# Hymba layer on one core: sums of weight blocks by adding DMAs instead of GpSimd operations, and roots by one GpSimd power

## Chip, cores and metric

The kernel runs on one core of a Trainium2 chip. The metric is the device time of one execution, in microseconds (us). The profile names the engines PE (TensorE; PEld is its weight loading), DVE (VectorE), ACT (ScalarE), POOL (GpSimd) and SP (SyncE, which here only issues DMAs).

## The reference, cut to what matters

One decoder layer for 1024 tokens of width 1024, in fp32: half a SwiGLU feed-forward network (FFN1), a mixer of a gated convolution and a diagonal state-space model (SSM), half a second FFN, each behind an RMSNorm with a shift, a scale and a gate from a condition vector.

```
x <- x + 1/2 * g1 * SwiGLU_1( adaLN_1(RMSNorm(x)) )          # d_ff = 2816
h  = adaLN_2(RMSNorm(x));  [b, c, v, u] = split(h @ W_in)
yA = b * conv3_causal(c * v)
yB = GLU( Re(C . state) + D*u ),  state_t = Abar state_{t-1} + Bbar u_t
x <- x + g2 * ( [RMSNorm(yA) | RMSNorm(yB)] @ W_out )
x <- x + 1/2 * g3 * SwiGLU_2( adaLN_3(RMSNorm(x)) )
y  = RMSNorm_final(x)

swiglu(h) = (silu(h @ w_gate) * (h @ w_up)) @ w_down
rms_norm(x) = x * rsqrt(mean(x * x) + 1e-6) * gain
```

## The kernel before

**Products.** Features lie on the 128 partitions, tokens on the columns in two halves of 512. Each fp32 operand is split into a high and a low part, and a product is three matmuls: high by high, high by low, low by high (`mm3`, 3 matmuls of 512 columns). A weight block of 128 x 1024 (512 KB, here called a granule) is split by ACT, which copies the high part, and DVE, which subtracts it (`w<-raw` in the profile). A granule feeds 24 matmuls in the FFNs.

**Seven instead of eight.** The FFN works in 11 groups of 256 hidden features. Most groups, and most of the down projection, are done as products of 2 x 2 blocks with seven block products instead of eight (`seven` for gate and up, `down7` for down). That is so for 9 groups of FFN1, 10 of FFN2, and 2 x 2 parts of the down projection in each FFN: 27 sets of seven. With left blocks A11, A12, A22 and sums of left blocks S1 to S4, the right operands are, of the four weight blocks of a set:

```
0: b11    1: b12 - b11    2: b22 - b12 + b11    3: b21
4: b22 - b12    5: b22    6: b21 - (b22 - b12 + b11)
```

Four of the seven are sums, and each takes one POOL operation over 128 x 1024 (lines 170, 171, 172 and 191). The first three are issued together, at the second granule of a set, from two raw tiles that hold two blocks each, partly in place; the fourth behind the split of the fifth granule. The tuple `SEVEN` gives the order of the products; banks B, C and A in PSUM collect them, and `copied`, `add`, `out` and `update` take them out by ACT and DVE.

**The weight stream.** `Weights` hands the granules out in a fixed list. SP loads raw tiles of 1 MB (two granules) into 2 buffers (`rawp`); split tiles go into a ring of 3 (`ringp`), with a fourth (`ring1`) at the head and in the mixer, where no `sums` tile is open. `pump` splits the next granule as soon as a tile of the ring is given back by `free`, and `ahead` loads the next raw tile when one is used up.

**The order.** All engines work off their instructions in order. The text of the kernel sets that order together with a scheduler that sorts by priority; `InOrder` (whose `call` is the line 112 of most instructions of PE, ACT, DVE and SP in the profile) ties each engine's instructions to the order in which they are written. `Clock` counts the `mm3` and lets side work in between them: in FFN1 the preparation of the SSM (`ssm_base`, `ssm_batch`: tables, and the kernels `kc` with the diagonal `dg` added, in 8 batches of 4 groups of channels), the modulation vectors (`wm`), and norms. `fa5gB` is bank B of gate in group 5 of FFN1, `fb0d` the down projection of group 0 of FFN2, `n_0` and `n_256` the halves of the last part of the final norm.

In the mixer a batch of the SSM goes through DVE (`X`, `sz`, `si`, `co`); `swx` and `swz` are pairs of small DMAs by SP that move states across partitions, and `yy` is the output on PE, which needs `co` after `swz` has landed.

**Roots.** `roots` makes 1/sqrt from sums of squares in a few columns per 128 tokens: a first guess from the bits (`ni`) and refinement, ten small DVE operations with the mean; `wide` spreads it over 128 columns times 0.375 (`rb`), and PE turns that into rows (`bc`). The squares themselves are added up by POOL in 8 pieces per norm (line 347).

Of the kernel before, what the change touches and what calls it, by code (L numbers as in the profile page):

```python
# [21 lines left out]
P = 128  # L22
# [22 lines left out]
PAD = 96, 100  # L45
# [10 lines left out]
ROOT_BITS, ROOT_A, ROOT_B = 1595932665.0, 0.703952253, 2.38924456  # L56
# [64 lines left out]
class Weights:  # L121
# [5 lines left out]
    def __init__(self, engines, srcs, granules, raw_bufs):  # L127
        self.V, self.A, self.SP, self.G = engines
        self.srcs, self.granules, self.raw_bufs = srcs, granules, raw_bufs
        self.left = [0] * len(srcs)  # L130
        for j, c, _ in granules:
            self.left[j] += c != "t4"
        self.raws, self.tiles, self.sums, self.kinds = [], [], {}, []
        self.given = self.freed = 0
        self.sums_pool = None
        self.slots = deque()

    @staticmethod
# [8 lines left out]
    def retire(self, pool):  # L147

        self.slots = deque(p for p in self.slots if p is not pool)
        self.kinds = [None if p is pool else p for p in self.kinds]  # L150
# [13 lines left out]
    def chunk(self, j, c, k):  # L164
        if isinstance(c, int):
            return self.raws[j][:, c, :]
        if c == "t1":
            f = self.sums[j] = self.sums_pool.tile([P, 1024], F32, tag="sums", name=f"sums{j}")
            b11, b12, b22 = self.raws[j][:, 0, :], self.raws[j][:, 1, :], self.raws[k][:, 0, :]
            self.G.tensor_tensor(out=f[:], in0=b22, in1=b12, op=ALU.subtract)  # L170
            self.G.tensor_tensor(out=b12, in0=b12, in1=b11, op=ALU.subtract)  # L171
            self.G.tensor_tensor(out=b11, in0=f[:], in1=b11, op=ALU.add)  # L172
        return {"t1": self.raws[j][:, 1, :], "t2": self.raws[j][:, 0, :]}.get(c, self.sums[j][:])

    def pump(self):
        while self.slots and len(self.tiles) < len(self.granules):
            i = len(self.tiles)
            j, c, k = self.granules[i]
            if self.sums_pool is None and c == "t1":
                return  # L180
            self.load((k if c == "t1" else j) + 1)
            src = self.chunk(j, c, k)
# [10 lines left out]
            self.left[j] -= c != "t4"  # L193
            self.ahead()

    def take(self, n=1):
        self.pump()
        got = self.tiles[self.given : self.given + n]
        assert len(got) == n
        self.given += n  # L200
        return got

    def free(self, n=1):
        for pool in self.kinds[self.freed : self.freed + n]:
            if pool is not None:
                self.slots.append(pool)
        self.freed += n
        self.pump()
# [9 lines left out]
def hymba_layer(ctx: ExitStack, tc, x_d, xt_d, wm1_d, wmod_d, gu1_d, gs1_d, ds1_d, wl1_d, win_d, wout_d, glu_d, gu2_d, gs2_d, wd2_d, ds2_d, wl2_d, cols_d, cond_d, lam_d, bc_d, out_d):  # L218
# [13 lines left out]
    ringp = pool("ringp", bufs=3, side="right")  # L232
    rawp = pool("rawp", bufs=2, side="right")
# [27 lines left out]
    V.memset(one[:], 1.0)  # L261
    mods = const.tile([P, 3, KT], F32, name="mods")
    scl = const.tile([P, 3, KT], F32, name="scl")
    gate = const.tile([P, 3, KT], F32, name="gate")

    srcs, granules = [], []

    def plain(arrays):
        for a in arrays:
            granules.extend((len(srcs), q, None) for q in range(2))  # L270
            srcs.append(a)

    def stream(gu, gs, wd, ds, wl, m):
# [4 lines left out]
        for g in range(m, NGRP):  # L278
            j = len(srcs)
            inner = g == 1  # L280
            srcs.extend([gs[g - m, 0], wd, gs[g - m, 1]] if inner else [gs[g - m, 0], gs[g - m, 1]])
            first, *rest = Weights.seven(j, j + 1 + inner)
            granules.extend([first, *([(j + 1, q, None) for q in range(2)] if inner else []), *rest])
        for c in range(CHUNKS):
            for p in range(2):
                granules.extend(Weights.seven(len(srcs), len(srcs) + 1))
                srcs.extend([ds[c, p, 0], ds[c, p, 1]])
# [5 lines left out]
    ws = Weights((V, A, SP, nc.gpsimd), srcs, granules, 2)  # L293
    ws.raw_pool = lambda i: rawp
# [79 lines left out]
    def roots(st, q, width, nm):  # L374

        v, y, a = (const.tile([P, 8], F32, tag=f"n{i}", name=f"{nm}n{i}", bufs=1)[:, :q] for i in "vya")
        yi = const.tile([P, 8], I32, tag="ni", name=nm + "ni", bufs=1)[:, :q]
        V.tensor_scalar(out=v, in0=st[:, :q], scalar1=1.0 / width, scalar2=EPS, op0=ALU.mult, op1=ALU.add)
        V.tensor_scalar(out=yi, in0=v.bitcast(I32), scalar1=-0.5, scalar2=ROOT_BITS, op0=ALU.mult, op1=ALU.add)
        src = yi.bitcast(F32)  # L380
        V.scalar_tensor_tensor(out=a, in0=src, scalar=-ROOT_A, in1=src, op0=ALU.mult, op1=ALU.mult)
        V.tensor_tensor(out=a, in0=a, in1=v, op=ALU.mult)
# [1482 lines left out]
```

## Time and profile before

| | |
|---|---|
| median of 3 runs | 1706.53 us (1703.99 to 1710.12) |
| profiled execution | 1708.08 us |
| its span in the trace | 1706.2 us, granted clock 0.991 |
| PE busy | 1668.5 us, 98% |
| DVE, ACT, POOL busy | 70%, 39%, 20% |
| the four sums on POOL, 27 times each | 70.0 + 73.7 + 71.9 + 66.6 us |
| DMA | 281.45 MB, 46% of the queues' time |

How to read the rows: in a row of the timeline the first number is the start in us after the span's start, the second the length (of a run of like instructions, with its count behind x), then the engine, the line, the operation, and out<-in with shapes. A bracket gives the idle time of the engine just ahead of it and what ended that. In rows of a window stand its bounds and length, busy time and count of PE, PEld, DVE, ACT and POOL, then PEclk, the clock that PE was granted (1.00 is full), then the DMA share and GB/s. Rows of grouped instructions end with busy us, mean ns of one, and the idle time before them.

### The profile page before, as it was taken

Reading aid. Unit: us, or ns where it says so; the run is one execution under the profiler, and the core shown is the slowest. Engines: PE = TensorE matmul, PEld = TensorE weight load, DVE = VectorE, ACT = ScalarE, POOL = GpSimd, SP = SyncE. Lnnn points to the kernel's source line nnn. Section 1 sums busy time; section 2 is a strip of 40 time slices with the busy share of each in tenths; the row PEclk is TensorE's granted clock in tenths of the full one; section 3 lists DMA queues with packets and bytes.
Section 4 is the critical chain, followed back from the end, with each engine's and each line's share of the span. In section 5 each row is a group of like instructions: output and inputs, shape, how many; then the busy total and the mean of one; then the engine's idle time right before and its main releaser. Section 6 shows DMA issues by size and latency. Waiting matters only on the chain.

```text
span 1706.2 us, 20362 instructions
## 1 busy us (share of the span) xinstructions
PE 1668.5 (98%) x7545; PEld 1373.4 (80%) x7545; DVE 1188.2 (70%) x1660; ACT 667.8 (39%) x983; POOL 341.2 (20%) x189
## 2 busy tenths in 40 slices
PE   8999999999999999999999999999999999999997
PEld 5888887788888888788777878788888888888886
DVE  7896788887598967725556848856666666555545
ACT  6526333333454332332114416434444444322233
POOL 1022221232223202100000020122222233222212
PEclk9999999999999999999999999999999999999998
DMA  9534554444765257145643233224434444839212
GB/s 352 191 118 141 190 200 152 154 148 151 271 219 176 96 198 265 50 111 152 198 154 120 87 111 128 95 87 173 185 148 177 168 161 160 332 147 382 101 50 99
DMA packets 101621, 281.45 MB, mean 165 GB/s; under 512 B 19345, under 2 KB 34961, under 8 KB 90386
## 3 DMA queue, kind: packets, MB, share of 16 engines
q1 hardware_dynamic: 101522, 280.15, 46.0%
q8 instruction: 59, 0.97, 0.2%
q14 instruction: 40, 0.33, 0.1%
HBM read 195.69 MB, written 76.02 MB: 159 GB/s over the span
## 4 chain that ended last, share of the span: by engine, by line
PE 68%; DVE 7%; DMA 4%; issue 1%; POOL 1%; ACT 1%; SPq 0%; DVEq 0%; POOLq 0%; ACTq 0%
PE wo L112 4%; PE fald L112 3%; PE fbd_1B L112 3%; PE fbd_0B L112 3%; PE fb10d L112 2%; PE u L112 2%; PE fad_1B L112 2%; PE fad_0B L112 2%; DMA swz<-si 2%; PE b L112 2%; DVE w L112 1%; PE fbd_1C L112 1%; PE fbd_0C L112 1%; PE c L112 1%; PE fad_1C L112 1%; PE fad_0C L112 1%
## 5 line engine op out<-in xcount | busy, mean ns | idle before, releaser
L112 DVE TENSOR_TENSOR w<-raw,w 128x1024 fp32r<-128x1024 f32 x185 | 244.9, 1325 | 158.4 <-ACT w L112 158.0
L112 ACT CAST w<-raw 128x1024 fp32r<-128x1024 f32 x185 | 194.1, 1050 | 263.7 <-PE v L112 35.0
L191 POOL TENSOR_TENSOR sums<-raw,raw 128x1024 f32<-128x1024 f32 x27 | 66.6, 2468 | 481.3 <-DVE w L112 481.3
L170 POOL TENSOR_TENSOR sums<-raw,raw 128x1024 f32<-128x1024 f32 x27 | 70.0, 2594 | 355.5 <-DMA raw<-in_gs 128.5
L112 DVE TENSOR_TENSOR w<-sums,w 128x1024 fp32r<-128x1024 f32 x54 | 66.0, 1222 | 71.6 <-ACT w L112 71.6
L112 DVE CUSTOM_DVE_ANT_0 wm<-wm,cact 128x1024 f32<-128x1024 f32 x56 | 81.1, 1463 | 22.3 <-DMA wm<-in_wmod 22.1
L172 POOL TENSOR_TENSOR raw<-sums,raw 128x1024 f32<-128x1024 f32 x27 | 71.9, 2661 | 51.3 <-DVE w L112 50.8
L171 POOL TENSOR_TENSOR raw<-raw 128x1024 f32<-128x1024 f32 x27 | 73.7, 2731 | 2.1
L112 ACT CAST w<-sums 128x1024 fp32r<-128x1024 f32 x54 | 56.7, 1050 | 43.6 <-PE fbd_1A L112 15.8
L347 POOL TENSOR_TENSOR n3aq<-n3aq,n3aq 128x512 f32<-128x512 f32 x5 | 8.6, 1716 | 277.0 <-ACT n3aq L112 276.9
L112 PE MATMUL p<-h,w 128*128 128x512 f32 x192 | 49.2, 406 | 2.2 <-ACT h L112 1.5
L112 PE MATMUL c<-h,w 128*128 128x512 f32 x192 | 48.1, 403 | 0.0
L112 PE MATMUL v<-h,w 128*128 128x512 f32 x192 | 46.9, 395 | 0.0
L112 PE MATMUL wo<-oa,w 128*128 128x512 f32 x192 | 45.5, 391 | 1.3 <-DVE w L112 0.7
L112 PE MATMUL b<-h,w 128*128 128x512 f32 x192 | 45.6, 393 | 0.0
L112 PE MATMUL wo<-ob,w 128*128 128x512 f32 x192 | 45.2, 391 | 0.0
L112 PE MATMUL u<-h,w 128*128 128x512 f32 x192 | 44.8, 392 | 0.2 <-DVE h L112 0.2
L112 PEld LDWEIGHTS p<-h,w 128*128 128x128 f32 x192 | 35.6, 191 | 10.2 <-ACT h L112 2.0
L112 PEld LDWEIGHTS wo<-oa,w 128*128 128x128 f32 x192 | 35.8, 188 | 9.4 <-DVE w L112 1.1
L112 PEld LDWEIGHTS c<-h,w 128*128 128x128 f32 x192 | 36.5, 194 | 7.3
L112 PEld LDWEIGHTS u<-h,w 128*128 128x128 f32 x192 | 35.7, 188 | 8.3 <-DVE h L112 0.6
L112 PEld LDWEIGHTS wo<-ob,w 128*128 128x128 f32 x192 | 35.8, 188 | 7.4
(1587 smaller groups left out, 4078.6 us busy)
## 6 DMA issues: line engine op xcount, KB each, us to landing
raw<-in_gs SPq DMA_DIRECT2D x38, 1024.0 KB, 5.0
wm<-in_wmod SPq DMA_DIRECT2D x56, 512.0 KB, 5.1
raw<-in_ds SPq DMA_DIRECT2D x16, 1024.0 KB, 4.9
mw<-in_wm SPq DMA_DIRECT2D x8, 1024.0 KB, 8.4
raw<-in_win SPq DMA_DIRECT2D x8, 1024.0 KB, 5.7
raw<-in_gu SPq DMA_DIRECT2D x6, 1024.0 KB, 4.8
raw<-in_wl SPq DMA_DIRECT2D x5, 1024.0 KB, 5.6
xb<-in_xt SPq DMA_DIRECT2D x8, 512.0 KB, 6.4
```

Of the source, the lines that this page charges most:

```text
L112: r = getattr(self.engine, name)(*args, **kw)
L170: self.G.tensor_tensor(out=f[:], in0=b22, in1=b12, op=ALU.subtract)
L171: self.G.tensor_tensor(out=b12, in0=b12, in1=b11, op=ALU.subtract)
L172: self.G.tensor_tensor(out=b11, in0=f[:], in1=b11, op=ALU.add)
L191: self.G.tensor_tensor(out=f, in0=self.raws[k][:, 1, :], in1=self.raws[j][:, 0, :], op=ALU.subtract)
L347: nc.gpsimd.tensor_tensor(out=a, in0=a, in1=sq[:, :n], op=ALU.add)
```

## The change

- The sums are made by DMAs issued from POOL's queue which add a block from memory to one that lies in SBUF (`add`, line 166 after the change). Only adding is used, so the signs are turned: the left sums S1, S2, S4 and the columns of the second half come with other signs (`joined` with `neg`, Silu with scale -1, `minus` gate for the updates of the upper half). A set of seven now splits at four places a block that is a sum (x = b11, then + b12; y = b12 + b22, then + b11, then + b21) and at three a raw block (b11, b22, b21). The granules are split in another order than they are used (`order`), and the products S4 and A12 change places in `SEVEN`.
- Raw tiles are single granules of 512 KB, 3 buffers; the ring has 4 tiles throughout; `ring1` and the `sums` pool go. The fourth raw tile at the head lies in another pool.
- `roots` is the mean on DVE and one POOL operation, pow with a tile of -0.5; `wide` multiplies by 1.0.
- `dg` and its addition to `kc` (two DVE operations a batch) become four operations of one group each.

```diff
-    def seven(j, k):
-        return [(j, 0, k), (j, "t1", k), (j, "t2", k), (k, 1, k), (j, "t3", k), (k, 0, k), (j, "t4", k)]
+    def seven(self, b, inner=()):
+        b11, b12, b22, b21 = (b[q] for q in range(4))
+        x = self.source(b11)
+        got = [self.granule(x, b12)]
+        self.order.append(got[0])
+        for src in inner:
+            self.plain(src)
+        y = self.source(b12, b22)
+        got += [self.granule(y, b11), self.granule(x), self.granule(y, b21)]
+        got += [self.granule(self.source(src)) for src in (b22, b21)]
+        got.append(self.granule(y))
+        self.order.extend(got[q] for q in (2, 3, 4, 1, 5, 6))
...
+    def add(self, r, src):
+        self.G.dma_start(out=r[:], in_=src, accum_op=ALU.add)
...
     def load(self, upto):
         while len(self.raws) < min(upto, len(self.srcs)):
             i = len(self.raws)
-            r = self.raw_pool(i).tile([P, 2, 1024], F32, tag="raw", name=f"raw{i}")
-            self.SP.dma_start(r[:], self.srcs[i])
+            r = self.raw_pool(i).tile([P, 1024], F32, tag="raw", name=f"raw{i}")
+            src, more = self.srcs[i]
+            self.SP.dma_start(r[:], src)
+            if more is not None:
+                self.add(r, more)
...
-    def chunk(self, j, c, k):
...
-            self.G.tensor_tensor(out=f[:], in0=b22, in1=b12, op=ALU.subtract)
-            self.G.tensor_tensor(out=b12, in0=b12, in1=b11, op=ALU.subtract)
-            self.G.tensor_tensor(out=b11, in0=f[:], in1=b11, op=ALU.add)
...
             self.A.copy(hi, src)
             self.V.tensor_tensor(out=lo, in0=src, in1=hi.bitcast(F32), op=ALU.subtract)
-            if c == "t3":
-                f = self.sums[j][:]
-                self.G.tensor_tensor(out=f, in0=self.raws[k][:, 1, :], in1=self.raws[j][:, 0, :], op=ALU.subtract)
+            if more is not None:
+                self.add(self.raws[j], more)
...
-    ringp = pool("ringp", bufs=3, side="right")
-    rawp = pool("rawp", bufs=2, side="right")
+    ringp = pool("ringp", bufs=4, side="right")
+    rawp = pool("rawp", bufs=3, side="right")
...
-    def roots(st, q, width, nm):
+    def roots(st, q, width, nm, y=None):
...
         V.tensor_scalar(out=v, in0=st[:, :q], scalar1=1.0 / width, scalar2=EPS, op0=ALU.mult, op1=ALU.add)
-        V.tensor_scalar(out=yi, in0=v.bitcast(I32), scalar1=-0.5, scalar2=ROOT_BITS, op0=ALU.mult, op1=ALU.add)
...
-        V.scalar_tensor_tensor(out=y, in0=a, scalar=5.0, in1=y, op0=ALU.add, op1=ALU.mult)
+        nc.gpsimd.tensor_tensor(out=y, in0=v, in1=power[:, :q], op=ALU.pow)
...
+    def joined(out, a, b, op, neg=False):
+        if neg:
+            V.scalar_tensor_tensor(out=out, in0=a, scalar=-1.0, in1=b, op0=ALU.mult, op1=op)
+        else:
+            V.tensor_tensor(out=out, in0=a, in1=b, op=op)
...
-    SEVEN = (("A11", "B"), ("S1", "C"), ("S2", "B"), ("A12", "A"), ("S3", "B"), ("S4", "C"), ("A22", "B"))
+    SEVEN = (("A11", "B"), ("S1", "C"), ("S2", "B"), ("S4", "C"), ("S3", "B"), ("A12", "A"), ("A22", "B"))
...
-                A.activation(t[:], src[:], AF.Silu)
+                A.activation(t[:], src[:], AF.Silu, scale=-1.0 if fi else 1.0)
...
-        dg = bt(f"dg{b}")
...
-        V.tensor_tensor(out=kc3[:, :, 0:CH], in0=kc3[:, :, 0:CH], in1=dg3, op=ALU.add)
+        for g in range(GB):
+            V.scalar_tensor_tensor(
+                out=kc3[:, g, 0:CH], in0=ident[:CH, :CH], scalar=ssm["lam"][:CH, 3, b * GB + g : b * GB + g + 1], in1=kc3[:, g, 0:CH], op0=ALU.mult, op1=ALU.add
+            )
```

More of the change, by code (lines that the diff above doesn't have):

```diff
@@ L177, in pump @@
             i = len(self.tiles)
[L178 to L182, printed above, removed]
+            j, more = self.granules[i]
+            self.load(j + 1)
+            src = self.raws[j][:]
             pool = self.slots.popleft()
@@ L197, in take @@
         self.pump()
-        got = self.tiles[self.given : self.given + n]
+        got = [self.tiles[i] for i in self.order[self.given : self.given + n]]
         assert len(got) == n
@@ L203, in free @@
     def free(self, n=1):
-        for pool in self.kinds[self.freed : self.freed + n]:
-            if pool is not None:
-                self.slots.append(pool)
+        for i in self.order[self.freed : self.freed + n]:
+            self.slots.append(self.kinds[i])
         self.freed += n
@@ L261, in hymba_layer @@
     V.memset(one[:], 1.0)
+    power = const.tile([P, 4], F32, name="power")
+    nc.gpsimd.memset(power[:], -0.5)
     mods = const.tile([P, 3, KT], F32, name="mods")
@@ L264, in hymba_layer @@
     gate = const.tile([P, 3, KT], F32, name="gate")
-    srcs, granules = [], []
+    minus = const.tile([P, 3, KT], F32, name="minus")
+    ws = Weights((V, A, SP, nc.gpsimd), 3)
     def plain(arrays):
         for a in arrays:
-            granules.extend((len(srcs), q, None) for q in range(2))
-            srcs.append(a)
+            for q in range(2):
+                ws.plain(a[:, q, :])
     def stream(gu, gs, wd, ds, wl, m):
@@ L704, in update @@
                 d = 2 * p + i + 4 * half
-                V.scalar_tensor_tensor(out=x[d][h], in0=src[:], scalar=gate[:, n_, d : d + 1], in1=x[d][h], op0=ALU.mult, op1=ALU.add)
+                by = (minus if half else gate)[:, n_, d : d + 1]
+                V.scalar_tensor_tensor(out=x[d][h], in0=src[:], scalar=by, in1=x[d][h], op0=ALU.mult, op1=ALU.add)
             def copied(dst, b, i, nm):
@@ L760, in sums_opened @@
         ws.pump()
-        return es, first
+        return first
     es1 = ExitStack()
@@ L804, in hymba_layer @@
     mod_load()
-    ws.load(1)
+    ws.load(2)
     b1 = cols[:, C_BMOD + SC1 * KT : C_BMOD + (SC1 + 1) * KT]
@@ L909, in hymba_layer @@
     mod_load()
-    ws.load(2)
+    ws.load(4)
     mod_load()
```

144 lines of the change are left out of this document (52 added, 92 removed).

## The prediction

> **What bounds the kernel now.** I read the page first, then the waits of PE, then PE's clock by windows around those waits, and last the timelines in them.
>
> ```profile
> PE 1668.5 (98%) x7545; PEld 1373.4 (80%) x7545; DVE 1188.2 (70%) x1660; ACT 667.8 (39%) x983; POOL 341.2 (20%) x189
> PE 68%; DVE 7%; DMA 4%; issue 1%; POOL 1%; ACT 1%; SPq 0%; DVEq 0%; POOLq 0%; ACTq 0%
> ```
>
> PE is busy nearly always, and the change takes no matmul away. POOL, whose work is removed, holds 1% of the chain. So the 20% of POOL are no measure of the gain: it can come only from stretches in which PE waits. These are the waits that the change can touch (us in total, times, longest):
>
> ```profile
> PE yy L112 <- DVE co L112: 6.1, 6, 2.9
> PE fb0d L112 <- DVE x L112: 3.3, 1, 3.3
> PE n_256bc L112 <- DVE n_256rb L112: 2.6, 1, 2.6
> PE n_0bc L112 <- DVE n_0rb L112: 2.4, 1, 2.4
> PE fa5gB L112 <- DVE fa5gc L112: 1.9, 1, 1.9
> PE fa6uB L112 <- DVE fa6uc L112: 1.9, 1, 1.9
> ```
>
> A wait costs more than its length. In the windows behind four of them the granted clock (PEclk, the column before the DMA share) is lower; the last row is an undisturbed one:
>
> ```profile
> 271.00:280.00 9.00, 7.87 (x28) 6.33 (x29) 8.90 (x14) 3.89 (x6) 2.41 (x1) 0.81 0.41 134
> 318.00:327.00 9.00, 7.10 (x24) 5.36 (x23) 8.96 (x13) 2.06 (x3) 2.38 (x1) 0.81 0.32 102
> 813.00:825.00 12.00, 9.09 (x35) 7.53 (x34) 2.95 (x5) 2.13 (x4) 0.00 (x0) 0.72 0.63 184
> 1102.00:1111.00 9.00, 8.82 (x32) 7.11 (x33) 6.81 (x11) 1.04 (x1) 0.00 (x0) 0.81 0.01 2
> 1111.00:1120.00 9.00, 9.00 (x41) 7.48 (x40) 4.94 (x6) 1.65 (x2) 0.00 (x0) 1.00 0.00 0
> ```
>
> At 0.81, 9 us lose 9 x 0.19 = 1.7 us; at 0.72, 12 us lose 12 x 0.28 = 3.4 us. I add these to the waits.
>
> Where the wait of fa5 comes from, the timeline shows (start, length, engine, operation):
>
> ```profile
> 264.63 2.88 PE L112 MATMUL fa5gC<-h1S,w 128*128 128x512 f32 x12
> 266.15 2.39 POOL L170 TENSOR_TENSOR sums<-raw,raw 128x1024 f32<-128x1024 f32 x1 [10.40 <-DMA raw<-in_gs]
> 266.39 2.22 DVE L112 TENSOR_TENSOR dg<-ident,lam 16x64 f32<-16x64 f32 x1 [2.84 <-DMA si_d<-rot]
> 267.35 2.88 PE L112 MATMUL fa5uC<-h1S,w 128*128 128x512 f32 x12
> 268.62 2.37 POOL L171 TENSOR_TENSOR raw<-raw 128x1024 f32<-128x1024 f32 x1
> 268.70 2.36 DVE L112 TENSOR_TENSOR kc<-kc,dg 16x64 f32<-16x64 f32 x1
> 271.31 0.68 DVE L112 TENSOR_TENSOR fa5gc<-fa5gc,fa5gB 128x512 f32<-128x512 f32 x1
> 272.13 4.29 PE L112 MATMUL fa5gB<-h,w 128*128 128x512 f32 x12 [1.91 <-DVE fa5gc L112]
> ...
> 246.82 0.20 DVE L112 TENSOR_TENSOR dg<-ident,lam 16x64 f32<-16x64 f32 x1
> ```
>
> The dg operation of 16x64 takes 0.20 us where POOL is idle and 2.22 us beside POOL's sum; twice a small DVE operation ends within 0.1 us of a POOL sum. While POOL reads its two blocks, such a DVE operation stands still, and fa5gc, which frees a PSUM bank for PE, comes behind it. The same at the start of FFN2:
>
> ```profile
> 1097.07 2.71 POOL L172 TENSOR_TENSOR raw<-sums,raw 128x1024 f32<-128x1024 f32 x1
> 1098.11 2.75 DVE L112 TENSOR_TENSOR w<-raw,w 128x1024 fp32r<-128x1024 f32 x1 [0.57 <-ACT w L112]
> 1101.39 0.74 DVE L112 SCALAR_TENSOR_TENSOR x<-fb0d,gate,x 128x512 f32<-128x512 f32 x1
> 1102.18 0.50 PE L112 MATMUL fb0d<-fb_1a,w 128*128 128x512 f32 x1 [3.25 <-DVE x L112]
> ```
>
> **The sums.** POOL's order, where the groups fa5 and fa6 are prepared (raw: a loaded block of weights; sums: POOL's own tile). Before:
>
> ```order
> L170 TENSOR_TENSOR sums_1999<-raw_1848,raw_1799 128x1024
> L171 TENSOR_TENSOR raw_1799<-raw_1799 128x1024
> L172 TENSOR_TENSOR raw_1799<-sums_1999,raw_1799 128x1024
> L191 TENSOR_TENSOR sums_1999<-raw_1848,raw_1799 128x1024
> L170 TENSOR_TENSOR sums_2354<-raw_2206,raw_2162 128x1024
> ```
>
> Now:
>
> ```order
> L166 DMA raw_1487<-in_gs 128x1024
> L166 DMA raw_1436<-in_gs 128x1024
> L166 DMA raw_1487<-in_gs 128x1024 x2
> L166 DMA raw_1796<-in_gs 128x1024
> L166 DMA raw_1743<-in_gs 128x1024
> ```
>
> Four sums became four adding transfers of 512 KB for each of 27 groups, 108 in all. POOL reads no block any more, so the three waits lose their cause. They are 1.9 + 1.9 + 3.3 = 7.1 us, and 3 x 1.7 = 5.1 us of clock: **-12.2**, and at worst 0. What is late next at fa5: dg and kc became four operations of this size, some 4 x 0.2 = 0.8 us from 266.39, and fa5gc could start by 267.5; PE asks for the bank 2.72 us after 267.35 (the distance of the two PE rows), at 270.07. That is 2.5 us of room.
>
> What an adding transfer takes, no row of before shows. The nearest are plain loads (KB each, us to landing; the last under the heaviest traffic, 1440 to 1500):
>
> ```profile
> raw<-in_gs SPq DMA_DIRECT2D x38, 1024.0 KB, 5.0
> wm<-in_wmod SPq DMA_DIRECT2D x56, 512.0 KB, 5.1
> ...
> fb2lS<-kept2S SPq DMA_DIRECT2D x4, 512.0 KB, 11.0
> ```
>
> I bound it by 5.1 and 11.0 and take 5.1 for most. The room: a granule is 24 matmuls, 2 x 2.72 = 5.44 us, a group 38.1. The tightest adds (b12 on x, b11 on y) lie between the splits of tiles two places apart in the order of production, 2 x 5.44 less some 2.5 us for the split by ACT and DVE (an estimate; DVE's part alone took 2.75 beside the sum above): 8.4 us. If one lasts longer, ACT and DVE wait with the split and all behind it; PE waits only after the granule that it has in hand as well, at 14 us, and at 17 us with the fourth ring tile (the old ring had three). So 5.1 is free, and 11.0 makes ACT late but not PE.
>
> Each add is also a new wait on POOL's queue: it stands there until its block has landed and ACT and DVE have read what was in it. Behind it are the next adds, and in the norms the additions of squares and pow; the norms' stages have few adds, and the end of the kernel none, so that I count nothing for it.
>
> **The mixer.** Raw loads are halved, and their place on SP's queue is another. Where the second half of the first SSM batch's state is moved across partitions (swz), before:
>
> ```order
> L112 DMA swx_6125<-X_6121 64x512 x2
> L112 DMA raw_6183<-in_win 128x2048
> L112 DMA swz_6136<-si_6037 64x512 x2
> L112 DMA mi_6209<-mi_d 128x512
> L112 DMA si_6268<-si_d 128x512
> ```
>
> Now:
>
> ```order
> L111 DMA swx_6151<-X_6147 64x512 x2
> L111 DMA raw_6209<-in_win 128x1024
> L111 DMA swz_6162<-si_6061 64x512 x2
> L111 DMA mi_6235<-mi_d 128x512
> L111 DMA si_6294<-si_d 128x512
> ```
>
> The load is still ahead of swz, but it is half as long, and with three buffers of one granule each its buffer is free a granule (5.44 us) before si, so that it should land before swz starts. What it cost (timeline, then the issues between 800 and 822):
>
> ```profile
> 808.66 0.33 SPq L112 DMA_DIRECT2D raw<-in_win  x1
> 809.26 1.10 SPq L112 DMA_DIRECT2D swz<-si  x2
> 816.11 0.69 DVE L112 TENSOR_TENSOR co<-co,swz 128x512 f32<-128x512 f32 x1 [2.84 <-DMA swz<-si]
> 816.86 0.79 PE L112 MATMUL yy<-co,mo 128*128 128x127 f32 x2 [2.91 <-DVE co L112]
> ...
> swz<-si SPq DMA_DIRECT2D x2, 128.0 KB, 6.3
> swx<-X SPq DMA_DIRECT2D x2, 128.0 KB, 2.6
> ```
>
> swz landed in 6.3 us behind the 1 MB, its twin swx in 2.6 us without it. The 3.7 us between them are more than the wait of 2.9, so the wait and its 3.4 us of clock can go: -6.3. The other five waits of yy (6.1 - 2.9 = 3.2 us) have no such load ahead in every case, and twice as many loads are issued; I take **-5**, between -9 and 0.
>
> **The roots.** The last one, at the end of the kernel:
>
> ```profile
> 1696.05 0.15 DVE L112 TENSOR_SCALAR n_256nv<-n_256st 128x2 f32<-128x2 f32 x1
> 1697.61 0.16 DVE L112 SCALAR_TENSOR_TENSOR n_256ny<-n_256na,n_256ny 128x2 f32<-128x2 f32 x1
> 1697.88 0.29 DVE L112 TENSOR_SCALAR n_256rb<-n_256ny 128x256 f32<-128x256 f32 x1
> ...
> L347 POOL TENSOR_TENSOR n_0q<-n_0q,n_0q 128x512 f32<-128x512 f32 x6 | 7.7, 1290 | 35.7 <-ACT n_0q L112 35.7
> L347 POOL TENSOR_TENSOR n_256q<-n_256q,n_256q 128x256 f32<-128x256 f32 x6 | 4.4, 738 | 4.8 <-ACT n_256q L112 4.8
> ```
>
> From nv's end, 1696.20, to rb's start lie 1.7 us; pow on POOL takes that place. POOL's adds are 1290 ns at 512 columns and 738 at 256, 2.2 ns a column and 0.2 us fixed; at two columns an add would be 0.2 us. A power may cost more: I take 0.8 us with both hand-overs, between 0.4 and 2.7 (a 1024-wide sum). Two roots stand before PE here (n_0 and n_256): 2 x 0.9 = **-1.8**, from -2.6 to +2. In the middle PE waits for none, and at the head the loads land last: nothing. The Trainium skill, GPSIMD Engine Reference, section 2.1 Instruction dispatch, says that the first call to a newly loaded GpSimd routine pays some 6 us of code loading; if pow were one, the head, not the tail, would give them back, and the sum would be 6 higher. No run here shows it.
>
> **Small debts.** The modulation's DVE operation is one place further ahead in the W_out stage (+1, about one such operation), 56.6 MB more are read, which lengthens other landings, and the first group of FFN2 has its adds within some us of their use. An estimate: **+4**, between 0 and 9.
>
> Sum: -12.2 - 5 - 1.8 + 4 = -15. The profiled execution took 1708.08 us, so 1693; the median of the runs is 1.55 lower than it, so I forecast **1691.5**. With the bounds: best -12.2 - 9 - 2.6, some 1683; all terms poor, about 1711.
>
> **The rivals.** (1) The waits stay though their cause is gone: dg waited 2.84 us for the landing of si_d, and the added traffic may make that later by what the lock took; FFN2's first splits may wait for their adds. For it: the DVE is full in these windows (8.90 of 9.00). Against it: the 2.5 us of room. Without the first term: 1691.5 + 12.2 = 1703.7, within the 0.3% (5.1 us) that a measurement of this kernel can tell from no change.
>
> (2) Slower: the adds land too late. An adding transfer has to read its target too, which may double it, and its descriptors come from POOL. It decides at 17 us for the mean add: from there every microsecond costs PE 27, one for each group, and 0.55 us eat the gain of 15. At 18 us the time is 1691.5 + 27 = 1718.5. Against it: twice 5.1 is 10.2. The Trainium skill, SBUF — State Buffer, section SBUF: two separate sides, speaks against this change: while VectorE runs certain operations GpSimd can't write a DMA's descriptors, and a DMA of 620 ns took 3100 ns beside one. By that rule each add comes some 2.5 us later, by an estimate 7.6 us, still under 17. No run here shows it.
>
> (3) pow is slow, 8 us or more for each. At 8 the two at the end give back the 1.8 us and cost 2 x (8 - 1.7) = 12.6 more: 1705.9; the norms between the stages, which have the same chain and now lie beside other work, then come late too, and their number puts it over 1711.7. For it speaks nothing in the trace but that no power is in it.
>
> (4) The edit does less than it says, since the splits (DVE, w from raw) become late in place of the sums: as (1).
>
> **How the numbers follow.** Forecast 0.62, with 1684 to 1699 for its own; more than that, since PE's small waits elsewhere also go, 0.05; rivals (1) and (4) 0.16, of which 0.03 faster; rival (2) 0.13; rival (3) 0.04, slower. Faster 0.62 + 0.05 + 0.03 = 0.70; within 0.3% 0.13; slower 0.17. The range goes from 1680 to 1711: rivals (2) and (3), 0.17, lie outside.
>
> **What would show it.** In the profile of after: no POOL sums; dg's successors at 0.2 us and no PE wait at fa5gB, fa6uB, fb0d; clock 1.00 there; swz of the first batch landing in under 4 us; one POOL operation of under 1 us between nv and rb. Wrong it is if PE waits for w tiles whose ACT copy waits for an adding transfer, in many groups, or if pow takes over 1.7 us.

## The result

The changed kernel takes 1698.31 us (median of 6 runs, 1695.89 to 1702.72) against 1706.60 us for the kernel before in the same comparison (6 runs). The ratio is 0.9946, with a 95% interval of 0.9929 to 0.9963: 0.5% faster, 8 to 9 us. The forecast was 1691.5 with a range of 1680 to 1711, so the direction and the range held and the gain was a little over half of the 15 us forecast. The profiled executions differ by 12.1 us (1708.08 and 1695.99, spans 1706.2 and 1694.2); the terms below are made against their spans. The runs of one kernel scatter by some 3 us to each side, so a stage that differs by 2 us in one profile proves little by itself.

### The profile page after: what moved, and what is told of

Read it like the earlier page. It is cut to its first block, busy times and chain, and to the rows that moved or that the text cites. A ratio compares the mean times of both kernels' runs of the same rounds, so it can differ in the third digit from the quotient of the medians.

```text
span 1694.2 us, 20669 instructions
## 1 busy us (share of the span) xinstructions
PE 1664.0 (98%) x7545; PEld 1370.0 (81%) x7545; DVE 1063.2 (63%) x1572; ACT 670.3 (40%) x983; POOL 165.2 (10%) x203
## 3 DMA queue, kind: packets, MB, share of 16 engines
q0 software_dynamic: 15552, 56.63, 19.3%
## 4 chain that ended last, share of the span: by engine, by line
PE 80%; DVE 8%; DMA 7%; ACT 2%; issue 1%; SPq 1%; POOL 0%; DVEq 0%; POOLq 0%; ACTq 0%
PE fald L111 4%; DMA wm<-in_wmod 3%; PE p L111 3%; PE fbd_1B L111 3%; PE fbd_0B L111 3%; PE fb10d L111 2%; PE fad_0B L111 2%; PE fad_1B L111 2%; PE wo L111 2%; PE b L111 2%; PE u L111 2%; PE fad_1C L111 1%; DMA swx<-X 1%; PE fbd_1C L111 1%; PE fbd_0C L111 1%
## 5 line engine op out<-in xcount | busy, mean ns | idle before, releaser
L111 DVE TENSOR_TENSOR w<-raw,w 128x1024 fp32r<-128x1024 f32 x239 | 292.5, 1226 | 248.3 <-ACT w L111 237.2
L111 ACT CAST w<-raw 128x1024 fp32r<-128x1024 f32 x239 | 250.9, 1051 | 305.0 <-DMA raw<-in_ds 59.4
L166 POOL DMA_DIRECT2D raw<-in_gs x76 | 66.7, 878 | 753.5 <-DVE w L111 425.9
L111 DVE CUSTOM_DVE_ANT_0 wm<-wm,cact 128x1024 f32<-128x1024 f32 x56 | 75.7, 1374 | 38.6 <-DMA wm<-in_wmod 38.6
L166 POOL DMA_DIRECT2D raw<-in_ds x32 | 28.0, 875 | 284.4 <-DVE w L111 162.5
L111 PEld LDWEIGHTS b<-h,w 128*128 128x128 f32 x192 | 35.7, 188 | 7.3
L111 PEld LDWEIGHTS v<-h,w 128*128 128x128 f32 x192 | 35.5, 188 | 7.1
L111 DVE SCALAR_TENSOR_TENSOR x<-fb10d,gate,x 128x512 f32<-128x512 f32 (+1 forms) x20 | 12.9, 643 | 24.4 <-PE fb10d L111 24.3
L111 PE MATMUL fb10d<-fb9lA,w 128*128 128x512 f32 (+1 forms) x120 | 25.6, 347 | 0.0
L111 DVE TENSOR_TENSOR X<-co,X 128x512 f32<-128x512 f32 x8 | 5.5, 693 | 31.5 <-DMA swx<-X 24.7
```

The costliest lines, as they stand in the source:

```text
L111: r = getattr(self.engine, name)(*args, **kw)
L166: self.G.dma_start(out=r[:], in_=src, accum_op=ALU.add)
```

## The profile after

The page, its first block and the DMA queues. The queue q0 is new: the adding DMAs' packets, MB and share of the 16 engines' time.

```profile
span 1694.2 us, 20669 instructions
PE 1664.0 (98%) x7545; PEld 1370.0 (81%) x7545; DVE 1063.2 (63%) x1572; ACT 670.3 (40%) x983; POOL 165.2 (10%) x203
...
q1 hardware_dynamic: 112898, 280.16, 47.7%
q0 software_dynamic: 15552, 56.63, 19.3%
```

POOL's share is halved and DVE's is 7 points lower, yet the span is only 12 us shorter. The DMA engines have 19.3% more to do. PE's waits:

```profile
PE fad_1C L111 <- ACT fad_1c L111: 2.9, 1, 2.9
PE yy L111 <- DVE co L111: 2.4, 3, 1.5
...
PE wo L111 <- ACT w L111: 2.2, 1, 2.2
...
PE n_256bc L111 <- DVE n_256rb L111: 1.4, 1, 1.4
...
PE fa6gB L111 <- DVE fa6gc L111: 1.0, 1, 1.0
PE fa4uB L111 <- DVE fa4uc L111: 0.8, 1, 0.8
```

fb0d, n_0bc and fa5gB have left the list, fa6uB fell from 1.9 to 0.8, yy from 6.1 to 2.4; `fad_1C`, in the down projection of FFN1, `wo` and fa4 are new or longer. The table gives the length of each stage in us, from the start of its first matmul to the start of the next stage's first, in the profiled execution of five kernels (the experiments are told below). A stage bears the name of its first product: fa2 is group 2 of FFN1, fad its down projection and fald the rest of that, px the first product of the SSM, gl its gate, wo the product with W_out, fb0 group 0 of FFN2.

| stage, from and to | before | after | no adds | short sums | loads behind swz |
|---|---|---|---|---|---|
| to fa2 | 119.95 | 119.18 | 118.83 | 119.65 | 119.80 |
| fa2 to fa5 | 114.24 | 117.40 | 114.24 | 114.24 | 114.40 |
| fa5 to fa7 | 90.57 | 84.89 | 82.52 | 82.67 | 92.79 |
| fa7 to fad | 158.85 | 158.64 | 158.64 | 158.82 | 158.85 |
| fad to fald, down projection of FFN1 | 153.02 | 158.21 | 152.32 | 152.32 | 153.00 |
| fald to px | 130.97 | 131.34 | 131.33 | 132.41 | 130.96 |
| px to wo, SSM and gate | 165.45 | 154.38 | 157.08 | 160.70 | 154.06 |
| wo to fb0 | 105.37 | 109.69 | 108.24 | 106.56 | 106.05 |
| fb0 to fb2 | 110.41 | 105.97 | 105.96 | 106.60 | 110.35 |
| fb2 to n_0bc, rest of FFN2 | 535.57 | 535.58 | 535.57 | 535.57 | 535.57 |
| n_0bc to n_256bc | 13.81 | 10.92 | 10.93 | 14.63 | 13.83 |
| span | 1706.20 | 1694.22 | 1682.76 | 1692.09 | 1697.67 |

Four stages give 24 us (fa5 to fa7 5.7, px to wo 11.1, fb0 to fb2 4.4, the tail 2.9), three take 13 back (fa2 to fa5 3.2, the down projection 5.2, wo to fb0 4.3).

## Experiments: what the sums cost, and what the adds cost

**POOL's sums alone.** The kernel before, its sums over 16 of 1024 columns, so that they are not made:

```diff
-            self.G.tensor_tensor(out=b12, in0=b12, in1=b11, op=ALU.subtract)
+            self.G.tensor_tensor(out=b12[:, :16], in0=b12[:, :16], in1=b11[:, :16], op=ALU.subtract)
```

(and so the other three; the sums' tile is one that is filled with zeros once).

> The kernel before with each of its POOL sums over 16 columns instead of 1024 (the sums are then not made); nothing else is changed. Theory (POOL stands in DVE's way): the waits of fa5, fa6 and fb0d go, and the clock behind them: 10 to 12 us lower than before, 1694 to 1697. Rival (DVE is late anyway, since it is full in those windows): dg takes 0.2 us, but PE still waits over 1 us in each of the three places, and the gain is under 4 us.

Measured: 1695.56 us, ratio 0.9930 (0.9915 to 0.9945), span 14.1 us shorter than before. fa5 to fa7 lost 7.9 us and fb0 to fb2 3.8; none of the three waits is in its list. POOL's operations did stand in DVE's way, and that cost some 12 us with the clock. The other 4.8 us are of the stage from px to wo, where no sum is made. They came with an earlier landing of swz (3.3 us instead of 3.9) in the same order; why it landed earlier no run shows.

**The adds alone.** The changed kernel without its adding transfers (the sums are not made), in the same order of instructions on all other queues:

```diff
-        self.G.dma_start(out=r[:], in_=src, accum_op=ALU.add)
+        pass
```

> The changed kernel with its 108 adding transfers left out (the sums are then not made; every other instruction stands in the same order). Theory (traffic): the 56.6 MB that the adds move make the kept blocks of the FFN1 down projection and the modulation's loads land late, and that is what the new waits of fa2, fa4, fa6 and of the down projection (the stage from fad to fald is 158.2 us against 153.0 before) come from. Then the stage is back at 153, fa2 to fa6 lose their new waits, and the time is 7 to 10 us lower than the changed kernel's 1698.3: 1688 to 1691. Rival (order): the new waits come from the changed order of the products and of the fetches; then the stage stays at 158 and the time within 2 us of 1698.

Measured: 1684.99 us, ratio 0.9871 (0.9855 to 0.9888), span 11.5 us shorter than the changed kernel's. fa2 to fa5, fa5 to fa7 and the down projection are 3.2, 2.4 and 5.9 us shorter; FFN2 doesn't change at all. The rival (order) fell, and the time is 3 us below the expected range: the adds cost 11.5 us, nearly all in FFN1. The run takes out two things at once, the adds' bytes and ACT's own waits for blocks with an add (59.4 us in total for the down projections' blocks and 15.3 for the others in the changed kernel; the list without the adds has neither), so it doesn't by itself show that the bytes are the cause. Windows of FFN1 (us, busy of PE, PEld, DVE, ACT and POOL, PEclk, DMA share, GB/s), before:

```profile
240.00:480.00 240.00, 235.90 (x1061) 191.95 (x1061) 191.53 (x245) 97.04 (x141) 59.38 (x23) 0.99 0.52 179
```

After:

```profile
240.00:480.00 240.00, 238.22 (x1090) 194.19 (x1089) 162.50 (x262) 96.19 (x138) 21.15 (x24) 1.00 0.83 231
```

After without the adds:

```profile
240.00:480.00 240.00, 240.00 (x1096) 196.56 (x1095) 165.87 (x263) 105.03 (x150) 0.00 (x0) 1.00 0.56 184
```

The DMA engines go from 0.52 to 0.83 busy with the adds, and what else is to land there lands later: the modulation's loads (`wm`) in 6.6 us with the adds and 5.4 without, by the DMA issues of the two kernels. DVE works off its instructions in order, so a `wm` operation that waits for its load holds up the emptying of a bank behind it, as at fa4 in the changed kernel:

```profile
230.64 1.23 DVE L111 CUSTOM_DVE_ANT_0 wm<-wm,cact 128x1024 f32<-128x1024 f32 x1 [0.84 <-DMA wm<-in_wmod]
...
232.99 0.68 DVE L111 TENSOR_TENSOR fa4uc<-fa4uc,fa4uB 128x512 f32<-128x512 f32 x1
...
233.73 2.56 PE L111 MATMUL fa4uB<-h,w 128*128 128x512 f32 x10 [0.81 <-DVE fa4uc L111]
```

At fa6 the profile has DVE wait for a transfer of the SSM (si_d from rott, 6.6 us to landing, 3.7 without the adds); the waits of fa2 were not followed up. In the down projection it is the kept blocks; the changed kernel's timeline there (the row with DMA is from the chain that ended last: issue and time to landing):

```profile
492.33 0.43 SPq L111 DMA_DIRECT2D fa4lA<-kept4X  x1
...
493.81 8.31 DMA fa7lA<-kept7X
...
499.91 0.62 ACT L111 CAST fa4lA<-fa4lA 128x512 fp32r<-128x512 f32 x1 [2.62 <-DMA fa4lA<-kept4X]
...
502.14 0.62 ACT L111 CAST fa7lA<-fa7lA 128x512 fp32r<-128x512 f32 x1
502.67 0.58 ACT L111 COPY fad_1c<-fad_1C 128x512 f32<-128x512 f32 x1
...
503.30 1.23 PE L111 MATMUL fad_1C<-fa1lS,w 128*128 128x512 f32 x3 [2.93 <-ACT fad_1c L111]
```

ACT stands 2.6 us before the first of four blocks that took 7.6 to 8.3 us to land; the last of them, fa7lA, sets the end of the row, and the copy that frees PE's bank comes behind it. The twelve matmuls behind that wait took 4.6 us instead of 2.7 (granted clock 0.86 from 496 to 508), so that wait and clock make up nearly all of the 5.2 us. The first three of the four landed in 5.2 to 5.4 us without the adds, where the wait is gone, and in 4.4 to 4.8 before.

**The order of the products.** Two kernels put A12 and S4 back to their old places, everywhere and in the down projections only, with b21 loaded ahead of b22 there:

```diff
-    SEVEN = (("A11", "B"), ("S1", "C"), ("S2", "B"), ("S4", "C"), ("S3", "B"), ("A12", "A"), ("A22", "B"))
+    SEVEN = (("A11", "B"), ("S1", "C"), ("S2", "B"), ("A12", "A"), ("S3", "B"), ("S4", "C"), ("A22", "B"))
...
-        got += [self.granule(self.source(src)) for src in (b22, b21)]
+        got += [self.granule(self.source(src)) for src in (b21, b22)]
```

> The changed kernel with the products A12 and S4 in their old places (and b21 and b22 loaded in the other order to match). Theory (traffic): the wait in the FFN1 down projection stays, the stage from fad to fald within 2 us of 158.2, time 1697 to 1700. Rival (order): with A12's kept blocks asked for where they were before, the stage is back at 153 to 154, and the time is 4 to 5 us lower.

> The changed kernel with the products A12 and S4 in their old places in the down projections only (b21 loaded ahead of b22 there). Theory: the FFN1 down projection's 5 us come from the adds' traffic meeting the fetch of A12's and A22's kept blocks, which the new order asks for close together; with the old order there the stage from fad to fald is 153 to 154, fa4 and fa5 stay as in the changed kernel, and the time is 1693 to 1695. Rival: the wait only moves within the stage (another bank or w is late): 157 or more, 1697 to 1699.

Measured: 1701.30 us (ratio 0.9964, 0.9947 to 0.9982) and 1701.51 us (0.9951, 0.9933 to 0.9970). With the old order everywhere the down projection took 153.8 us, as the rival had it, but fa4 to fa5 took 43.9 instead of 39.5, and nothing was won. With it in the down projections only the stage took 157.5: PE waited for another copy (`fad_0B` for ACT's `fad_0u`, 2.6 us). The second run's theory failed, and its rival held for the stage. But fa4 to fa5 took 42.5 in it too, though the order of the gate and up products is the changed kernel's there, so the lengths at fa4 can't be put down to that order. In the down projection the order decides which bank is late; neither old order was faster.

**How near the adds are to being the bound.** The changed kernel with every add made twice, and with only the add on x made twice (27 more; the sums are then others):

```diff
-        self.G.dma_start(out=r[:], in_=src, accum_op=ALU.add)
+        for _ in range(2):
+            self.G.dma_start(out=r[:], in_=src, accum_op=ALU.add)
```

```diff
             if more is not None:
                 self.add(self.raws[j], more)
+                if self.srcs[j][1] is None:
+                    self.add(self.raws[j], more)
```

> The changed kernel with each adding transfer made twice in a row (the sums are then others). Theory (traffic, with the room that the prediction worked out): two adds in a row land in 12 to 15 us, under the 14 to 17 us that PE can wait, so that the ordinary sets keep 38.08 us, and only the stages with much other traffic lose, about as much again as the first adds cost: 1708 to 1716. Rival (adds are the bound): the room is smaller than worked out; the ordinary sets grow over 40 us each, 27 times, and the time is 1750 or more.

> The changed kernel with only the one add on x made twice in each set, 27 adds more; in the run in which all 108 adds were made twice the sets took 55 us instead of 38. Theory (chain on y): a set's bound is y's own chain, one load, three adds and three splits, 5 + 3 x 6.4 + 3 x 2.5 = 32 us alone and 51 to 55 with doubled adds; x has one add only, and two still fit: FFN2's sets stay at 38.08 and the time is 1698 to 1706. Rival (rate: POOL or the DMA engines can't make that many adds): a quarter of the 385 us come back, 1780 or more. Rival (the room of x is used up like y's): each set grows by the 6 us of an add, less what is free: 1740 to 1800.

Measured: 2093.08 us (ratio 1.2232, 1.2185 to 1.2279) and 1734.99 us (1.0162, 1.0145 to 1.0179). With all adds twice a set of FFN2 takes 55.1 us (fb9 to fb10) instead of 38.08, by and large as the first run's rival had it, and ACT waits for blocks with an add all the time (us in total, times, longest):

```profile
ACT w L111 <- DMA raw<-in_gs: 491.9, 68, 12.3
ACT w L111 <- DMA raw<-in_ds: 258.2, 32, 13.8
```

The single add on x twice left the gate and up sets of FFN2 at 38.08, as its theory had it, and as this window shows, in which PE never stops:

```profile
1180.00:1420.00 240.00, 240.00 (x1061) 198.79 (x1060) 139.14 (x180) 107.60 (x156) 27.18 (x31) 1.00 0.87 238
```

So neither POOL nor the DMA engines are short of rate there (0.87 busy; with all adds twice they are less busy, 0.77 from 1500 to 1700), and the chain that I then wrote down for y fits: a load of 4.8 us, three adds, and three splits of 1.05 + 1.22 us (ACT's cast and DVE's subtraction). That is 4.8 + 3t + 6.8 us for a set, 38.08 at t = 8.8. With the adds twice, at the 7.5 us each and 5.4 for the load that its DMA issues show, it gives 5.4 + 45 + 6.8 = 57.2, and 55.1 were measured. That the two agree supports the chain; no run took one add out of it. The time of that run missed all three expectations (1698 to 1706, 1780 or more, 1740 to 1800): FFN1 and both down projections lost some 35 us even with x alone, 9.2 of them in FFN2's down projection, which one add more can make late though a single one doesn't. An add lands in 6.4 us (median of the 76 in the FFN groups; rows of the profile's page):

```profile
raw<-in_gs SPq DMA_DIRECT2D x76, 512.0 KB, 4.8
raw<-in_gs POOLq DMA_DIRECT2D x76, 512.0 KB, 6.4
...
raw<-in_ds SPq DMA_DIRECT2D x32, 512.0 KB, 4.9
raw<-in_ds POOLq DMA_DIRECT2D x32, 512.0 KB, 7.6
```

It is 1.6 us more than a plain load of the same size in the gate and up groups and 2.7 in the down projection. That the chain did not lengthen FFN2's sets, and so decide the result, was luck of 1.2 us (7.6 against 8.8) to 2.4 us.

## Experiments: the mixer

The kernel before, its weight loads in the mixer tied behind the last swz:

```diff
-            self.SP.dma_start(r[:], self.srcs[i])
+            got = self.SP.dma_start(r[:], self.srcs[i])
+            if self.behind is not None:
+                self.SP.follow(got, self.behind)
...
         sw = swapped(si, b, "swz")
+        ws.behind = SP.last
```

> The kernel before with one change of order on SP's queue: in the mixer each 1 MB weight load goes out behind the pair swz that it stood ahead of. Theory (queue): swz lands in 2 to 3 us instead of 6.3, PE's waits for co of 1.7 and 2.9 us fall under 1, and the stage from px to gl, 150.2 us, becomes 143 to 146; time 1700 to 1703. Rival (traffic): the load is still there at the same time and swz shares the DMA engines with it; then swz lands as late and the stage stays over 148.

Measured: 1698.85 us, ratio 0.9939 (0.9919 to 0.9960). That is a little better than the theory had it (1700 to 1703). px to wo is 11.4 us shorter, as much as in the changed kernel (11.1), by the place of four loads on a queue; three of them stood directly ahead of a swz, which then took 5.4 to 6.4 us to land. fa5 to fa7, where nothing was edited, came out 2.2 us longer in this profile. The third batch's swz and the load, in this kernel:

```profile
804.65 1.11 SPq L112 DMA_DIRECT2D swz<-si  x2
...
807.77 0.34 SPq L112 DMA_DIRECT2D raw<-in_win  x1
```

The issues between 765 and 910 (KB each, us to landing), before:

```profile
swx<-X SPq DMA_DIRECT2D x16, 128.0 KB, 2.6
swz<-si SPq DMA_DIRECT2D x16, 128.0 KB, 3.9
```

With the loads behind:

```profile
swx<-X SPq DMA_DIRECT2D x16, 128.0 KB, 3.4
swz<-si SPq DMA_DIRECT2D x16, 128.0 KB, 2.3
```

In the changed kernel:

```profile
swx<-X SPq DMA_DIRECT2D x16, 128.0 KB, 4.5
swz<-si SPq DMA_DIRECT2D x16, 128.0 KB, 2.2
```

The transfer that is late is now swx, ahead of which the loads went, and PE has other work until that is needed. The rival, that swz shares the DMA engines with the load wherever it stands, fell.

The same edit in the changed kernel:

> The changed kernel with the edit of the loads behind swz. In it the load that stands directly ahead of the first batch's swz is the only one that still does, and PE still waits 1.7 us for that batch's co. Theory (queue): that wait falls under 1 us, the stage from px to gl goes from 141.4 to 138 to 140, and the time is 1695 to 1697, below both kernels. Rival: the wait is there because the batch is late anyway: the stage stays at 141 and the time at 1698.

Measured: 1697.37 us, ratio 0.9929 (0.9909 to 0.9948). The first batch's wait for co fell from 1.5 to 0.5 us, as the theory had it, but the longest of the others is now 1.0, and px to gl went only from 141.4 to 140.7; the time can't be told from the changed kernel's.

## Experiments: the roots

The changed kernel with the roots on DVE; the second time with the pad smaller by 16 columns, so that the two small tiles which the old roots need (64 bytes) shift no pool behind them:

```diff
-PAD = 96, 84
+PAD = 96, 68
...
-        nc.gpsimd.tensor_tensor(out=y, in0=v, in1=power[:, :q], op=ALU.pow)
+        V.tensor_scalar(out=yi, in0=v.bitcast(I32), scalar1=-0.5, scalar2=ROOT_BITS, op0=ALU.mult, op1=ALU.add)
...
+        V.scalar_tensor_tensor(out=y, in0=a, scalar=5.0, in1=y, op0=ALU.add, op1=ALU.mult)
```

> The changed kernel with its roots by the ten DVE operations of before, which also puts the modulation's DVE operations in the W_out stage back to where they stood. Theory: pow is worth the tail's 2.9 us (the last root from 1.7 us between nv and rb to 0.8), and the moved modulation operation costs the W_out stage 4 us (109.7 against 105.4 us from wo to fb0g): the tail is 2.5 to 3 us longer, W_out about 4 shorter, the time 1697, within 2 us of the changed kernel. Rival: the W_out stage is longer for another reason (its loads, the ring): then it stays at 109 to 110 and the time is 1701.

> The changed kernel with the roots on DVE as in the run with DVE roots, but with the pad at the right edge of SBUF 16 columns (64 bytes) smaller, so that every tile lies where it does in the changed kernel. Theory (address): the two added small tiles shifted all others by 64 bytes, and that alone made each set of seven 38.45 us long instead of 38.08; now the sets are back at 38.08 (fa7 to fa8 41.24) and the time is 1701 to 1705: 3 us in the tail, some 2 at the last gate of the mixer. Rival (DVE): the ten operations hold up DVE everywhere; then fa7 to fa8 stays at 41.6 and the time at 1715 or more.

Measured: 1718.91 us (ratio 1.0063, 1.0048 to 1.0079) and 1710.82 us (1.0009, 0.9996 to 1.0021). Both missed: the first by 22 us, the second by 6 to 10. Of the first miss some 8 us were the address (last section), and W_out stayed long in it (111.8), as the rival had it. The second showed no single place: fa4 to fa5 2.3, px to gl 2.4, W_out 1.1 us longer beside the tail's 2.9, with the other order that the scheduler then makes; fa4 to fa5 differs as much between other kernels with adds (39.5 to 43.9). So with DVE's roots the changed kernel is no faster than the kernel before, and why its roots are worth some 11 us in it by the ratios, against 2.9 in the tail, is not shown. Pow by itself, and without any adds, is shown by the kernel before with the loads behind swz and pow:

> The kernel before with two changes: its mixer loads behind swz, as in the run that took 1698.9 us, and the roots by POOL's pow; POOL's sums stay. It shows what pow is worth without the adds. Theory: 2.9 us at the end of the kernel and some 1 us at the last gate of the mixer: 1694 to 1696. Rival (what the run with DVE roots showed, 12 us, is pow's): 1687 to 1689.

Measured: 1696.02 us, ratio 0.9933 (0.9919 to 0.9948), against 0.9939 without pow: the intervals overlap, so no gain in the whole is shown. The tail fell by 2.9 us (13.83 to 10.92); the rival, 12 us, fell here. W_out grew from 106.05 to 108.80 us in it. The changed kernel's tail:

```profile
1684.87 0.16 DVE L111 TENSOR_SCALAR n_256nv<-n_256st 128x2 f32<-128x2 f32 x1 [0.78 <-PE n_256st L111]
1685.11 0.71 POOL L381 TENSOR_TENSOR n_256ny<-n_256nv,power 128x2 f32<-128x2 f32 x1 [1.75 <-DVE n_256nv L111]
1685.85 0.29 DVE L111 TENSOR_SCALAR n_256rb<-n_256ny 128x256 f32<-128x256 f32 x1 [0.23 <-POOL n_256ny L381]
1686.20 0.71 PE L111 MATMUL n_256bc<-ident,n_256rb 128*128 128x128 f32 x4 [1.37 <-DVE n_256rb L111]
```

From nv's end to rb's start are 0.82 us, where 1.7 were.

**dg and kc on POOL.** To that kernel one edit more, which should take the waits of fa5 and fa6 without any add:

```diff
-        V.tensor_tensor(out=kc3[:, :, 0:CH], in0=kc3[:, :, 0:CH], in1=dg3, op=ALU.add)
+        nc.gpsimd.tensor_tensor(out=kc3[:, :, 0:CH], in0=kc3[:, :, 0:CH], in1=dg3, op=ALU.add)
```

(and dg's multiplication likewise).

> The same kernel with the two small operations dg and kc of each SSM batch moved from DVE to POOL, behind whose sums they stood still. Theory (POOL's sum holds up DVE operations with two inputs in SBUF): the waits at fa5 and fa6 go without any adding transfer, and the stages fa5 to fa6 and fa6 to fa7 fall from 45.1 and 45.5 us to about 41.5; 7 to 8 us less than the kernel without this edit, 1686 to 1689. Rival: the next DVE operation stands still in their place, or the sums come late behind dg: less than 3 us.

Measured: 1699.55 us, ratio 0.9951 (0.9934 to 0.9969), no gain; fa5 to fa7 is 95.1 us against 94.2, and PE waits 2.7 us at fa5 and 5.1 at fa6. The rival held, and the timeline at fa6 shows it:

```profile
315.88 2.41 POOL L174 TENSOR_TENSOR sums<-raw,raw 128x1024 f32<-128x1024 f32 x1 [12.16 <-DMA si_d<-rot]
316.40 2.04 DVE L112 TENSOR_TENSOR bb<-prm,qq 128x128 f32<-128x128 f32 x1 [5.00 <-DMA si_d<-rott]
318.26 0.33 POOL L1239 TENSOR_TENSOR dg<-ident,lam 16x64 f32<-16x64 f32 x1
318.56 2.33 POOL L175 TENSOR_TENSOR raw<-raw 128x1024 f32<-128x1024 f32 x1
320.86 0.31 POOL L1245 TENSOR_TENSOR kc<-kc,dg 16x64 f32<-16x64 f32 x1
321.20 0.29 DVE L112 TENSOR_TENSOR bb<-prm,qq 128x128 f32<-128x128 f32 x1 [2.75 <-POOL kc L1245]
```

The next small DVE operation, bb, stands still in dg's place (2.04 us, where its twin takes 0.29), and DVE then waits for kc behind POOL's second sum.

## Why the prediction was right, and where not

Against the spans the change gave 12.0 us where the sum had 15. The gains were 7.5 us more than forecast (12.5 at the sums without what the adds took back there, 11.1 in the mixer, 2.9 in the tail: 26.5 against 19), the debts 11 more (fa2 to fa5 3.2, fa6 2.4, down projection 5.2, W_out 4.3: 15.1 against 4); the other stages give 0.6. That the total came near was luck: two misses of opposite sign. The upper end of the range, 1711, is also not what its terms give; with all of them poor they make 1706.5 + 2 + 9, some 1717.5.

- **The sums, -12.2.** Right in kind and size: some 12 us in the three places with the sums cut short. In the changed kernel fa5 to fa7 and fb0 to fb2 gave 10.1; the adds took 2.4 back at fa6. The room at fa5 was overestimated, as the changed kernel's timeline shows:

```profile
270.14 0.29 DVE L111 TENSOR_TENSOR bb<-prm,qq 128x128 f32<-128x128 f32 x1 [2.33 <-DMA prm<-in_bc]
270.35 0.66 DVE L111 SCALAR_TENSOR_TENSOR kc<-ident,lam,kc 16x16 f32<-16x16 f32 x4
270.94 0.67 DVE L111 TENSOR_TENSOR fa5gc<-fa5gc,fa5gB 128x512 f32<-128x512 f32 x1
...
272.42 1.75 PE L111 MATMUL fa5gB<-h,w 128*128 128x512 f32 x7
```

  The four kc operations take 0.16 us each, but they start at 270.35 and not at 266.39, since DVE waited for the landing of a table. That is rival (1)'s mechanism; fa5gc was done 0.8 us before PE came, and it cost nothing. That was luck of 0.8 us: in the changed kernel with the loads behind swz, whose edit touches nothing here, the same table landed in 6.9 us instead of 5.3, and PE waited:

```profile
272.12 0.29 DVE L111 TENSOR_TENSOR bb<-prm,qq 128x128 f32<-128x128 f32 x1 [3.94 <-DMA prm<-in_bc]
...
273.73 3.01 PE L111 MATMUL fa5gB<-h,w 128*128 128x512 f32 x12 [2.44 <-DVE fa5gc L111]
```

- **The small debts, +4.** This is the step that failed, by size: the adds with their 56.6 MB alone cost 11.5 us, more than the end of the range given for all the debts (9), and W_out came on top. I had asked whether an add lands in time for its own split, and not what its traffic does to the transfers that DVE and ACT wait for in order: `wm`, the SSM's transfers and the kept blocks of FFN1, where the DMA engines were already half busy.
- **The mixer, -5.** It gave 11.1, of which 8.7 from px to gl, where swz is, and 2.4 behind it at the gate. The mechanism was right, and the loads' place alone gives as much (10.2 and 1.2). But the rows of the order that I quoted were of the first batch and the timeline of the third. In the first the load is still issued 0.6 us ahead of swz (779.74 and 780.34), against the argument that its buffer would be free a granule before, and PE waits 1.5 us there; in the third it has gone behind. The clock behind that stage came back too: 0.97 from 800 to 900 before, 1.00 after.
- **The roots, -1.8.** 2.9 in the tail. The fixed part was well judged: 0.71 us at two columns, between the 0.2 of an add and the 2.7 of a whole sum. The Trainium skill (GPSIMD Engine Reference, section 2.1 Instruction dispatch) says that the first call to a newly loaded routine pays some 6 us. The first pow started 0.15 us after its input was done and took 1.02 us, and those after it 1.01 to 1.43 at four columns: pow is no such call here.
- **W_out, +1.** The stage lost 4.3. A `wm` operation ahead of an update of x took 2.29 us beside POOL's addition of squares, where it took 1.22 before, and ACT's next split stands behind that update; PE's wait there went from 0.6 to 2.2 us:

```profile
990.33 1.22 DVE L112 CUSTOM_DVE_ANT_0 wm<-wm,cact 128x1024 f32<-128x1024 f32 x1 [1.19 <-DMA wm<-in_wmod]
```

```profile
984.08 2.29 DVE L111 CUSTOM_DVE_ANT_0 wm<-wm,cact 128x1024 f32<-128x1024 f32 x1 [1.31 <-DMA wm<-in_wmod]
...
988.75 5.43 PE L111 MATMUL wo<-oa,w 128*128 128x512 f32 x16 [2.23 <-ACT w L111]
```

  Two waits for `ob` (0.6 and 0.5 us) are new beside it. With pow in the kernel before it lost 2.75 of that, with DVE's roots in the changed kernel it stayed long as well (110.8). What share of the 4.3 is the order and what the landing of `wm` stays open.
- **Rival (2)**, the late adds, was priced with a point of 17 us, which its own working doesn't give (8.4 + 5.44 is 13.8, and one granule more 19.3). By the chain on y it lies near 8.8 us, since three adds follow each other on the same block y, and the room had been worked out for each as if the others cost nothing. The adds came at 6.4 to 7.6, so the rival didn't happen in FFN2; with the right point it deserved more than 0.13. The Trainium skill (SBUF — State Buffer, section SBUF: two separate sides) has a GpSimd-issued DMA of some 620 ns take some 3100 ns beside a VectorE copy; the estimate of 2.5 us more for each add was worked out from that. The adds are 1.6 to 2.7 us later than plain loads here, but whether for the descriptors or for reading the target no run tells apart.

Of the kernels that make the whole result the fastest four lie together at 0.993 to 0.995 of the time before: the change, the change with its loads behind swz, and the kernel before with four loads moved, with and without pow, with no adding DMA at all. Their intervals overlap. The 12 us of the sums and the 11.5 of the adds nearly cancel.

## What to carry to other kernels

Work that leaves an engine for the DMA queues is priced twice: by whether it lands in time, along the whole chain of transfers on one buffer and not for each by itself, and by what the added transfers do to every other landing that an engine waits for in order. Before taking an engine's work away, cut it short without replacement and measure that: here it showed some 12 us to be had at the sums, and the replacement spends 11.5. And look at the order on the DMA queue first: four large loads ahead of small transfers on which PE waits were worth as much as the whole change.

## What the runs showed of the hardware

Two kernels whose instructions are the same, the two with roots on DVE, differ by 1% in PE's rate at a full granted clock; in one the pools on SBUF's right side, the split weights' among them, lie 64 bytes further in. The same 270 us of FFN2, shifted and not shifted:

```profile
1150.00:1420.00 270.00, 270.00 (x1182) 221.50 (x1181) 155.96 (x203) 123.74 (x175) 24.36 (x28) 1.00 0.79 219
```

```profile
1150.00:1420.00 270.00, 270.00 (x1193) 223.56 (x1192) 159.28 (x209) 125.54 (x179) 25.22 (x29) 1.00 0.79 220
```

PE never idles in either and gets through 1182 and 1193 matmuls; a set of seven takes 38.45 and 38.08 us. No PE wait and no clock shows it. The run with the old order of products, on the same chip as the shifted one, has 38.08 us too, so it is not the chip. It rests on one pair of kernels, and which operand's address matters the runs don't tell. An edit that adds a small tile is better timed with the addresses kept, or it may be charged with time that is not its own: here 8 us, 0.5% of the kernel.
